# Residual stream with tokens on partitions, tokens stationary in all linears but the mixers' inputs, seven products in part of both MLP matmuls

## The chip, the core and the metric

One Trainium2 core runs the whole program: TensorE (PE, with its weight loads as PEld), VectorE (DVE), ScalarE (ACT), GpSimd (POOL) and the DMA queues of SyncE (SP) and ACT. The metric is the device time of one launch in microseconds, the median of three runs. One further execution was profiled; all rows below are of that one.

## The reference

256 tokens of width 2048 go through two layers. Layer 0 mixes with a recurrent unit and a pooling mixer, layer 1 with sparse attention; after each mixer stand an MLP of width 8192 and a gated addition. Everything is float32.

```python
def rmsnorm(x, g):
    y = x * rsqrt(mean(x * x, axis=-1) + EPS)
    return y * g

for i in range(2):
    hn = rmsnorm(h, ln_mix_g[i])
    h = h + (ab_mixer(hn, ...) if i == 0 else nsa_mixer(hn, ...))   # each ends in "@ w_out", 2048 x 2048
    hn = rmsnorm(h, ln_mlp_g[i])
    h = h + square(relu(hn @ mlp_w_up[i])) @ mlp_w_down[i]          # 2048 x 8192, 8192 x 2048
    gate = sigmoid(rmsnorm(h, ln_ple_g[i]) @ ple_w_gate[i])         # 2048 x 2048
    h = h + gate * (p[i] @ ple_w_proj[i])                           # 256 x 2048
return rmsnorm(h, ln_final_g)
```

## The kernel before

**Precision.** A float32 operand is written as a rounded `hi` part and the rest `lo`, and a product is taken as hi·hi + lo·hi + hi·lo in the fast float32 mode. Activations are kept as such pairs (`X(k)`, feature block k on partitions, 256 columns of hi then 256 of lo). Weights arrive raw by DMA, 1 MB a tile (`raw`, three buffers); ACT makes `hi` (L190) and DVE makes `lo` (L197), four buffers each.

**Order.** Nothing is scheduled by a tool. The list `steps` holds the PE's work in order. A step is one half of a raw tile: 2 x 512 columns of weights for 128 rows each. `run` goes through the steps. At step s it first issues the conversions to `hi` up to s+2, then the PE's matmuls of s, then whatever other code has put down with `after(n, f)` for this step (n steps after the one that called it), then the conversions to `lo` up to s+2. Every engine works through its own queue in that order, so an instruction put down by `after(0, ...)` stands ahead of `lo` of step s+2 in DVE's queue.

**Linears.** `linear` keeps a block of 128 x 128 weights stationary and streams tokens: per block one matmul of `hi` weights over 512 columns (hi and lo of the tokens, L284) and one of `lo` weights over 256 (L285), or in packed groups three of 256 (L280). Its results have features on partitions, as has the residual `h`; `Sums` adds the two halves of a bank, and `residual`, `gate_done` and `up` bring them into `h`, `X` and `H`. `x_stages` makes the next `X` from `h` with the squares for the norm; `rstd_soon` sums these over partitions with a matmul against ones (L364).

**MLP.** The 8192 hidden features go in four quarters q. `up(q)` makes 2048 hidden features with `linear`. `down(q, n2, B)` multiplies them into one half n2 of the outputs, with tokens stationary and 512 columns of weights streamed (L730 to L732, three matmuls a product: hi·hi, lo·hi, hi·lo); its results have tokens on partitions and are gathered in `D`. A pair p is 256 of the hidden features. Six of the eight pairs of a quarter take eight products, in two steps of four (`plain`). Two pairs, called own pairs (3 and 5, in the last quarter 4 and 6), are done with seven products (Q1, Q2, P3, Q5, P7, P6, P4) in four steps of one, two, two and two; DVE forms their weight sums (L758, L763, L764) and the sums of `H` (L700). Four PSUM banks collect the plain products (Q2, P3, P4, C4), four the own ones. When the second own pair is through, `own_out` brings the own banks together in four parts, `out1` to `out4`, one to four steps later; when pair 7 is through, `plain_out` adds the four plain banks to `D` one step later:

```python
                        if p == own[-1] and what[0][0] == "P6":
                            for d, g in enumerate(own_out):
                                after(1 + d, g)
```

After the last quarter `ends` turns `D` by 32 PE transposes a layer (L823) and adds it to `h`.

**Gated addition.** `ple` projects p[i] (packed), then runs the gate's linear; `gate_done` scales, takes tanh on ACT and adds on DVE, column group by column group. At the end of layer 1 `final_stages` and `finish` normalise and write the output.

## Time and profile before

| | |
|---|---|
| runs | 2317.48, 2317.49, 2317.65 us, median 2317.49 |
| profiled execution | 2317.87 us, its span 2315.9 us, so 1.97 us lie around the span |
| PE busy, matmuls | 2288.9 us (99%), 13218 |
| PE weight loads | 2006.2 us (87%) |
| DVE busy | 1722.1 us (74%) |
| ACT busy | 1238.7 us (53%) |
| DMA | 433.65 MB, 187 GB/s on average |
| PE waits for others, all | 15.0 us, of these 6.4 at the start |
| granted TensorE clock | 0.998 on average |

A busy time is the sum of what the profile gives each instruction; matmuls follow each other before the one ahead has ended, so their durations overlap and their pace is read from the starts. A window row gives busy time of each engine in a stretch and in brackets how many instructions began or ran in it. DVE's instructions overlap their neighbours a little too, so their pace also is read from starts.

### The profile page before, as it was taken

The page shows a single profiled execution, that of the slowest core. Times are in us where ns is not written, and L with a number is a line of the kernel's source. Part 1 is how long each engine was busy: PE and PEld are TensorE (multiplying, and loading weights), DVE is VectorE, ACT ScalarE, POOL GpSimd, SP SyncE. Part 2 cuts the span into 40 slices and gives each one's busy share as a digit, 9 for nine tenths or more (in the row PEclk, how much of TensorE's full clock was granted, in tenths as well). Part 3 has the DMA queues.
Part 4 walks back from the last instruction along what each step waited for, and adds up shares of the span by engine and source line. Part 5 has one row for each costly group of instructions (what it writes and reads, how often), then busy time and mean ns, then how long its engine had stood idle before and what let it go on. Part 6 is the DMA issues. An engine that isn't in the chain of part 4 may idle for free.

```text
span 2315.9 us, 33830 instructions
## 1 busy us (share of the span) xinstructions
PE 2288.9 (99%) x13218; PEld 2006.2 (87%) x13218; DVE 1722.1 (74%) x2660; ACT 1238.7 (53%) x1889; POOL 21.7 (1%) x44
## 2 busy tenths in 40 slices
PE   8999999999999999999999999999999999999997
PEld 8998988888888888899889988888888888888896
DVE  6786778768768768977875676767767767857977
ACT  6664555445544545665564555545445445445565
POOL 2000000000000000000000000000000000000000
PEclk9999999999999999999999999999999999999999
DMA  7445455555555555555775224555555555555453
GB/s 261 170 164 194 176 199 200 199 184 200 191 191 196 188 191 187 172 198 203 261 267 182 82 83 165 199 187 191 202 189 184 201 192 187 200 186 194 167 200 110
DMA packets 73360, 433.65 MB, mean 187 GB/s; under 512 B 9968, under 2 KB 18544, under 8 KB 23536
## 3 DMA queue, kind: packets, MB, share of 16 engines
q1 hardware_dynamic: 68640, 426.99, 52.1%
q10 hardware_dynamic: 4560, 4.51, 0.6%
q8 instruction: 103, 1.69, 0.3%
q14 instruction: 57, 0.47, 0.1%
HBM read 429.37 MB, written 2.10 MB: 186 GB/s over the span
## 4 chain that ended last, share of the span: by engine, by line
PE 96%; DVE 2%; issue 0%; ACT 0%; DMA 0%; SPq 0%; DVEq 0%; ACTq 0%
PE ps L284 30%; PE ps L280 17%; PE ps L285 15%; PE ps L732 9%; PE ps L731 9%; PE ps L730 9%; PE ps L1160 1%; PE ps L950 1%; DVE lo L197 1%; DMA raw<-in_ab_w_in 0%; PE ps L1102 0%; PE ps L1100 0%; PE ps L562 0%; PE ps L493 0%; PE ps L1103 0%
## 5 line engine op out<-in xcount | busy, mean ns | idle before, releaser
L190 ACT ACTIVATE hi<-raw 128x1024 fp32r<-128x1024 f32 (+2 forms) x825 | 842.1, 1024 | 756.2 <-PE ps L284 387.0
L197 DVE TENSOR_TENSOR lo<-raw,hi 128x1024 fp32r<-128x1024 f32 (+2 forms) x825 | 964.1, 1178 | 366.3 <-ACT hi L190 365.3
L284 PE MATMUL ps<-big,hi 128*128 128x512 f32 x3008 | 1059.7, 398 | 0.0
L285 PE MATMUL ps<-big,lo 128*128 128x256 f32 x3008 | 841.3, 280 | 0.7 <-DVE lo L197 0.5
L284 PEld LDWEIGHTS ps<-big,hi 128*128 128x128 f32 x3008 | 564.8, 188 | 137.0
L285 PEld LDWEIGHTS ps<-big,lo 128*128 128x128 f32 x3008 | 567.1, 189 | 2.4 <-DVE lo L197 1.5
L280 PE MATMUL ps<-big,hi 128*128 128x256 f32 x2304 | 426.1, 287 | 6.4 <-ACT hi L190 6.4
L732 PE MATMUL ps<-lo,big 128*128 128x512 f32 x992 | 386.3, 389 | 3.1 <-DVE lo L197 3.1
L730 PE MATMUL ps<-hi,big 128*128 128x512 f32 x992 | 386.8, 390 | 0.0
L731 PE MATMUL ps<-hi,big 128*128 128x512 f32 x992 | 386.0, 389 | 0.0
L280 PEld LDWEIGHTS ps<-big,hi 128*128 128x128 f32 x2304 | 362.0, 192 | 8.7 <-ACT hi L190 6.4
L280 PE MATMUL ps<-big,lo 128*128 128x256 f32 x1152 | 327.3, 284 | 2.6 <-DVE lo L197 2.6
L280 PEld LDWEIGHTS ps<-big,lo 128*128 128x128 f32 x1152 | 221.2, 192 | 3.7 <-DVE lo L197 3.6
L732 PEld LDWEIGHTS ps<-lo,big 128*128 128x128 f32 x992 | 186.2, 188 | 42.6 <-DVE lo L197 3.9
L730 PEld LDWEIGHTS ps<-hi,big 128*128 128x128 f32 x992 | 186.2, 188 | 38.6
L731 PEld LDWEIGHTS ps<-hi,big 128*128 128x128 f32 x992 | 186.2, 188 | 38.2
L190 ACT ACTIVATE hi<-T 128x1024 fp32r<-128x1024 f32 x64 | 67.9, 1061 | 103.1 <-PE ps L731 99.2
L197 DVE TENSOR_TENSOR lo<-T,hi 128x1024 fp32r<-128x1024 f32 x64 | 78.1, 1223 | 58.8 <-ACT hi L190 58.8
L308 ACT ACTIVATE t<-ps 128x256 f32<-128x256 f32 x156 | 57.9, 371 | 31.2 <-PE ps L285 31.2
L321 DVE TENSOR_TENSOR t<-ps,t 128x256 f32<-128x256 f32 x156 | 65.4, 419 | 1.5 <-ACT t L308 1.5
L386 ACT ACTIVATE big<-t 128x256 fp32r<-128x256 f32 x136 | 54.4, 401 | 6.7 <-DVE t L687 3.8
L687 DVE SCALAR_TENSOR_TENSOR t<-t 128x256 f32<-128x256 f32 x128 | 54.4, 425 | 4.4
(205 smaller groups left out, 1317.3 us busy)
## 6 DMA issues: line engine op xcount, KB each, us to landing
raw<-in_mlp_w_up SPq DMA_DIRECT2D x128, 1024.0 KB, 4.8
raw<-in_mlp_w_down SPq DMA_DIRECT2D x128, 1024.0 KB, 4.7
raw<-in_c_w_in SPq DMA_DIRECT2D x36, 1024.0 KB, 4.9
raw<-in_ple_w_gate SPq DMA_DIRECT2D x28, 1024.0 KB, 4.9
raw<-in_ab_w_in SPq DMA_DIRECT2D x20, 1024.0 KB, 4.8
raw<-in_ab_w_out SPq DMA_DIRECT2D x16, 1024.0 KB, 4.7
raw<-in_c_w_out SPq DMA_DIRECT2D x16, 1024.0 KB, 4.8
raw<-in_c_cmp_w_k SPq DMA_DIRECT2D x8, 1024.0 KB, 4.8
```

What stands on the lines that cost most here:

```text
L190: act.activation(halves[s]["hi"][:, k, :w], halves[s]["src"][:, k, :], AF.Copy)
L197: dve.tensor_tensor(lo[:, k, :w], src[:, k, :], halves[s]["hi"][:, k, :w].bitcast(F32), op=OP.subtract)
L280: pe.matmul(b, lhsT=wt[:, kk, cols], rhs=x[:, x0:x0 + T], start=first and n == 0 and j % 2 == 0, stop=last and n == 2, skip_group_check=True)
L284: pe.matmul(b, lhsT=hi[:, kk, cols], rhs=x, start=first, stop=False, skip_group_check=True)
L285: pe.matmul(b[:, T:], lhsT=lo[:, kk, cols], rhs=x[:, :T], start=False, stop=last, skip_group_check=True)
L308: act.activation(self.t[j], self.banks[j][:, T:], AF.Copy)
L321: dve.tensor_tensor(dst, self.banks[j][:, :T], self.t[j], op=OP.add)
L386: act.activation(dst[:, :T], src, AF.Copy, **kw)
L687: dve.scalar_tensor_tensor(ts.t[j], ts.t[j], 0.0, ts.t[j], op0=OP.max, op1=OP.mult)
L730: pe.matmul(b, lhsT=x_hi, rhs=hi[:, n, :], start=r not in begun, stop=False, skip_group_check=True)
L731: pe.matmul(b, lhsT=x_lo, rhs=hi[:, n, :], start=False, stop=False, skip_group_check=True)
L732: pe.matmul(b, lhsT=x_hi, rhs=lo[:, n, :], start=False, stop=end, skip_group_check=True)
```

## The change

`h` now has tokens on partitions (`[128, 2, 2048]`), and every linear but the mixers' input projections is done as `down` was: tokens stationary, 512 weight columns streamed, by `mm_set`, one call for each half n2 of 2048 output columns. The mixers' output projections, the gate and the projection of p use plain pairs only. Both MLP matmuls use own pairs, now 2 and 3 of each set of eight, in the order `ORDER` = 0, 1, 4, 5, 2, 6, 3, 7. `D` is gone: `h_out` adds each set's results to `h` right away, scaled by the per-token factor `R2`. What feeds the next matmul has to be turned: `x_after` turns `h` into `X`, `up_out` turns the squared hidden values, and for the first half the sums of its own pairs, into `H` and `S`, by PE transposes (`turn`, `s_back`). The norms' sums come from ACT's squares with an accumulated sum instead of DVE additions and a matmul. In `plain` the loops over n and t are exchanged. The weights are stored in the new blocks, the DMAs stay 1 MB each; `x` is also loaded a second time, 2 MB in the new layout on ACT's queue at step 20, and the final gains once, spread to all partitions.

```diff
--- before.py
+++ after.py
...
+    def mm_set(src, order, X, post, own=(), S=None, between={}, hooks={}):
...
+        def plain(p, k):
+            def fn(hi, lo):
+                for n in range(2):
+                    for t in range(2):
+                        product(PLAIN[t][n], A(p, k, t), hi, lo, n, k == 1 and p == order[-1])
+                if k == 1 and p == order[-1]:
+                    post(w.get("w"), [[acc_of(PLAIN[t][n]) for n in range(2)] for t in range(2)])
+            return fn
...
+                    if p == owned[-1] and what[0][0] == "P6":
+                        for d, g in enumerate((out1, out2, out3)):
+                            after(d, g)
...
+            return [(0, 1, None, fn(("Q1", lambda: A(p, 0, 0)))),
+                    (2, 2, None, fn(("Q2", lambda: A(p, 1, 0)), ("P3", 4))),
+                    (0, 2, first, fn(("Q5", 1), ("P7", 3))),
+                    (0, 2, second, fn(("P6", 2), ("P4", lambda: A(p, 1, 1))))]
...
+        def out1():
...
+            dve.tensor_tensor(w1[:, 1], acc_of("P6"), w1[:, 0], op=OP.subtract)
...
+        def out2():
+            w1, w2 = w["w"]
+            dve.scalar_tensor_tensor(w2[:, 0], w2[:, 0], -1.0, w1[:, 1], op0=OP.mult, op1=OP.subtract)
+            dve.tensor_tensor(w1[:, 1], w1[:, 1], w2[:, 1], op=OP.subtract)
...
+        def out3():
+            w1, w2 = w["w"]
+            dve.scalar_tensor_tensor(w2[:, 1], w2[:, 0], -1.0, w2[:, 1], op0=OP.mult, op1=OP.subtract)
...
+            parts = own_fns(p) if p in own else [(0, 2, None, plain(p, 0)), (2, 2, None, plain(p, 1))]
...
+    def turn(banks, i, of):
+        b = scratch(banks, i)
+        for j in range(2):
+            for t in range(2):
+                pe.transpose(b[:, j, t * P:(t + 1) * P], of(t, i // 2, (2 * i + j) % 4), ident)
...
+    SUM_PAIRS = (2, 3)
+    ORDER = (0, 1, 4, 5, 2, 6, 3, 7)
+    def h_out(n2, r, X, gi, sx=None, w_first=True):
+        def post(w, banks):
...
+            def wide(t):
...
+                    dve.scalar_tensor_tensor(ht, w[t], r[:, t:t + 1], ht, op0=OP.mult, op1=OP.add)
...
+            def adds(n):
+                for t in range(2):
...
+                        dve.scalar_tensor_tensor(hb(t, n), banks[t][n], r[:, t:t + 1], hb(t, n), op0=OP.mult, op1=OP.add)
+            if w is not None:
+                after(0, lambda: (wide(0), wide(1)))
+            after(0, lambda: adds(0))
+            after(0, lambda: adds(1))
+            if X is not None:
+                x_after(n2, banks, X, gi, sx)
...
+    def x_after(n2, banks, X, gi, sx=None, at=0):
...
+        def back(n):
+            for i in (2 * n, 2 * n + 1):
+                turn(banks, i, lambda t, n, c: hb(t, n)[:, c * P:(c + 1) * P])
...
+        def high(i):
...
+                split_hi(X(k), scratch(banks, i)[:, j], scale=gain(k))
...
+        def low(i):
...
+                dve.scalar_tensor_tensor(X(k)[:, T:], scratch(banks, i)[:, j], gain(k), X(k)[:, :T].bitcast(F32),
+                                         op0=OP.mult, op1=OP.subtract)
...
+        for n in range(2):
+            after(at + 1 + n, lambda n=n: back(n))
+            for i in (2 * n, 2 * n + 1):
+                after(at + 1 + n, lambda i=i: high(i))
+                after(at + 2 + n, lambda i=i: low(i))
+            after(at + 2 + n, lambda n=n: squares(n))
+        if sx is not None and n2 == 0:
+            after(at + 2, lambda: (keep(2), keep(3)))
+            after(at + 4, sums)
+            after(at + 5, s_high)
+            after(at + 5, s_low)
...
+            mm_set(lambda p, n2=n2: w[n2][p], order, Y, h_out(n2, None, X, gi, LazyS(0)))
...
+        def up_out(q, n2):
+            def post(w, banks):
+                W = w or wtiles()
...
+                def adds(n):
+                    for t in range(2):
+                        if w:
+                            dve.tensor_tensor(W[t][:, n], banks[t][n], W[t][:, n], op=OP.add)
...
+                def relu(n):
+                    for t in range(2):
+                        act.activation(W[t][:, n], W[t][:, n] if w else banks[t][n], AF.Relu)
+                    for t in range(2):
+                        act.activation(W[t][:, n], W[t][:, n], AF.Square)
...
+                def back(n):
+                    for i in (2 * n, 2 * n + 1):
+                        turn(banks, i, lambda t, n, c: W[t][:, n, c * P:(c + 1) * P])
...
+                def high(i):
+                    k = 2 * i
+                    act.activation(Hs[n2][:, k:k + 2, :T], scratch(banks, i), AF.Copy)
...
+                def low(i):
+                    k = 2 * i
+                    dve.tensor_tensor(Hs[n2][:, k:k + 2, T:], scratch(banks, i), Hs[n2][:, k:k + 2, :T].bitcast(F32),
+                                      op=OP.subtract)
...
+                def sums():
...
+                def s_back(i):
...
+                        pe.transpose(b[:, o], ph["f"][:, i, o], ident)
...
+                def s_split(i):
...
+                for n in range(2):
+                    after(n, lambda n=n: (adds(n), relu(n)))
+                    after(1 + n, lambda n=n: back(n))
+                    for i in (2 * n, 2 * n + 1):
+                        after(2 + n, lambda i=i: high(i))
+                        after(2 + n, lambda i=i: low(i))
+                if n2 == 0:
+                    after(3, sums)
+                    for i in range(2):
+                        after(4, lambda i=i: s_back(i))
+                        after(5, lambda i=i: s_split(i))
...
+        for q in range(4):
+            for n2 in range(2):
...
+                mm_set(lambda p, q=q, n2=n2: a["mlp_w_up"][l][q][n2][p], ORDER, X, post, SUM_PAIRS, LazyS(0))
+            for n2 in range(2):
+                mm_set(lambda p, q=q, n2=n2: a["mlp_w_down"][l][n2][8 * q + p], ORDER, H,
+                       h_out(n2, R2, Xn if q == 3 else None, G_PLE + 16 * l), SUM_PAIRS, LazyS(1))
...
-        def own_pairs(q):
-            return (3, 5) if q < 3 else (4, 6)
...
-                stages(4, [ts.copy, put, lambda j: split_hi(H(j0 + j), ts.t[j]), lambda j: split_lo(H(j0 + j), ts.t[j])],
-                       at=1)
...
-            linear(W("mlp_w_up", l), q * D, [4] * 4, X, done, packed=[0] if q == 0 else [])
...
-                    for t in range(2):
-                        for n in range(2):
-                            r = PLAIN[t][n]
-                            product(r, A(p, k, t), hi, lo, n, k == 1 and p == last[r])
-                    if k == 1 and p == KD // 2 - 1:
-                        after(1, plain_out)
...
-                        if p == own[-1] and what[0][0] == "P6":
-                            for d, g in enumerate(own_out):
-                                after(1 + d, g)
...
-                        dve.tensor_tensor(Dn(t)[:, n], Dn(t)[:, n], acc_of(PLAIN[t][n]), op=OP.add)
-                if q == 3:
+                        act.activation(e[:, t, n2 * 1024 + n * 512:n2 * 1024 + (n + 1) * 512], banks[t][n], AF.Copy, scale=0.5)
...
+        def gate(n2):
+            def post(w, banks):
+                W = wtiles()
...
+                def tanh(n):
+                    for t in range(2):
+                        act.activation(W[t][:, n], banks[t][n], AF.Tanh, scale=HALF[:, t:t + 1])
...
+                def add(n):
+                    for t in range(2):
+                        e = st["e"][:, t, n2 * 1024 + n * 512:n2 * 1024 + (n + 1) * 512]
+                        dve.scalar_tensor_tensor(W[t][:, n], W[t][:, n], 1.0, e, op0=OP.add, op1=OP.mult)
+                        dve.tensor_tensor(hb(t, n), hb(t, n), W[t][:, n], op=OP.add)
+                for n in range(2):
+                    after(at, lambda n=n: tanh(n))
+                    after(at, lambda n=n: add(n))
+                if l == 0:
+                    x_after(n2, banks, Xn, G_MIX + 16, at=at)
...
-                    ends(n2, [acc_of(r) for r in PLAIN[0] + PLAIN[1]])
...
-            def tanh(j):
-                act.activation(ts.t[j], ts.t[j], AF.Tanh, scale=0.5)
...
-            def add(j):
-                hk = h[:, j0 + j, :]
-                dve.scalar_tensor_tensor(ts.t[j], ts.t[j], 1.0, st["e"][:, j0 + j, :], op0=OP.add, op1=OP.mult)
-                dve.scalar_tensor_tensor(hk, ts.t[j], 0.5, hk, op0=OP.mult, op1=OP.add)```

In the orders below `lo<-raw,hi` is one conversion of a raw tile's half, `lo<-T,hi` or `lo<-big,hi` one of a weight sum.

DVE at the end of a `down` set before: the last `lo<-T` belong to the second own pair; L789 and L790 are `out2`, L793 and L794 `out3`, L798 `out4`, L804 `plain_out`; `w_3907` is the buffer `w`.

```order
L197 TENSOR_TENSOR lo<-T,hi 128x1024 x2
L197 TENSOR_TENSOR lo<-raw,hi 128x1024 x3
L789 TENSOR_TENSOR u<-ps,u 128x512
L790 SCALAR_TENSOR_TENSOR w_3907<-w_3907,u 128x512
L197 TENSOR_TENSOR lo<-raw,hi 128x1024
L793 TENSOR_TENSOR u<-u,w_3907 128x512
L794 SCALAR_TENSOR_TENSOR w_3907<-w_3907 128x512
L197 TENSOR_TENSOR lo<-raw,hi 128x1024
L798 TENSOR_TENSOR big<-big,u 128x1024
L798 TENSOR_TENSOR big<-big,w_3907 128x1024
L197 TENSOR_TENSOR lo<-raw,hi 128x1024
L804 TENSOR_TENSOR big<-big,ps 128x512 x4
```

DVE at the same place now: L210 is the conversion to `lo`, L760 is in `out1`, L764 and L765 are `out2`, L769 `out3`, L809 `wide`, L816 `adds`.

```order
L210 TENSOR_TENSOR lo<-big,hi 128x1024 x2
L210 TENSOR_TENSOR lo<-raw,hi 128x1024
L760 TENSOR_TENSOR u<-ps,u 128x512
L210 TENSOR_TENSOR lo<-raw,hi 128x1024
L764 SCALAR_TENSOR_TENSOR big<-big,u 128x512
L765 TENSOR_TENSOR u<-u,big 128x512
L210 TENSOR_TENSOR lo<-raw,hi 128x1024
L769 SCALAR_TENSOR_TENSOR big<-big 128x512
L809 SCALAR_TENSOR_TENSOR h<-u,rs,h 128x1024
L809 SCALAR_TENSOR_TENSOR h<-big,rs,h 128x1024
L816 SCALAR_TENSOR_TENSOR h<-ps,rs,h 128x512 x4
L210 TENSOR_TENSOR lo<-raw,hi 128x1024 x7
```

The first reader of the own banks stood behind three conversions after the own pair's; now it stands behind one, and everything up to the additions into `h` lies ahead of the third conversion after it.

DVE at the end of a gate set now (L1003 and L1004 are `add`, L845 makes the low part of the next `X`):

```order
L210 TENSOR_TENSOR lo<-raw,hi 128x1024 x5
L1003 SCALAR_TENSOR_TENSOR u<-u,big 128x512
L1004 TENSOR_TENSOR h<-h,u 128x512
L1003 SCALAR_TENSOR_TENSOR big<-big 128x512
L1004 TENSOR_TENSOR h<-h,big 128x512
L1003 SCALAR_TENSOR_TENSOR u<-u,big 128x512
L1004 TENSOR_TENSOR h<-h,u 128x512
L1003 SCALAR_TENSOR_TENSOR big<-big 128x512
L1004 TENSOR_TENSOR h<-h,big 128x512
L210 TENSOR_TENSOR lo<-raw,hi 128x1024 x2
L845 SCALAR_TENSOR_TENSOR big<-ps,gains,big 128x256 x4
```

Before, the gate's additions of 256 columns each (L867, L868) stood with one conversion between every two or three of them; now eight of 512 columns stand together ahead of one.

PE at the end of an `up` set (L703 to L705 are the three matmuls of a product, L787 the transposes):

```order
L703 MATMUL ps<-hi,big 128x512
L704 MATMUL ps<-hi,big 128x512
L705 MATMUL ps<-lo,big 128x512
L787 MATMUL ps<-ident,u 128x128
L787 MATMUL ps<-ident,big 128x128
L787 MATMUL ps<-ident,u 128x128
L787 MATMUL ps<-ident,big 128x128
L787 MATMUL ps<-ident,u 128x128
L787 MATMUL ps<-ident,big 128x128
L787 MATMUL ps<-ident,u 128x128
L787 MATMUL ps<-ident,big 128x128
L703 MATMUL ps<-hi,big 128x512
```

Eight transposes stand between two steps, and twice so at the end of each set that is turned; before, `up` had none.

## Rows read from the trace of the kernel before

**Rows 1.** The page: PE over the span, granted clock by fortieths of it

```profile
PE 2288.9 (99%) x13218; PEld 2006.2 (87%) x13218; DVE 1722.1 (74%) x2660; ACT 1238.7 (53%) x1889; POOL 21.7 (1%) x44
...
PEclk9999999999999999999999999999999999999999
```

**Rows 2.** Windows, a quarter's up, then its down: busy us (instructions), clock, DMA

```profile
428.59:519.03 90.44, 90.44 (x514) 78.39 (x512) 57.84 (x82) 42.58 (x59) 0.00 (x0) 1.00 0.54 193
519.03:603.38 84.35, 84.35 (x375) 69.83 (x374) 70.62 (x81) 45.01 (x54) 0.00 (x0) 1.00 0.55 192
```

**Rows 3.** Timeline of PE in a packed group: start, us, instruction

```profile
2285.55 0.28 PE L280 MATMUL ps<-big,lo 128*128 128x256 f32 x1
...
2285.91 0.28 PE L280 MATMUL ps<-big,lo 128*128 128x256 f32 x1
```

**Rows 4.** Timeline of PE at four transposes after a down set

```profile
919.45 0.60 PE L823 MATMUL ps<-ident,big 128*128 128x128 f32 x4
919.80 0.48 PE L730 MATMUL ps<-hi,big 128*128 128x512 f32 x1
920.12 0.40 PE L731 MATMUL ps<-hi,big 128*128 128x512 f32 x1
```

**Rows 5.** Timeline of PE in attention, the third and last of eight transposes

```profile
1392.72 0.27 PE L1140 MATMUL ps<-ident,big 128*128 128x128 f32 x1
...
1393.27 0.27 PE L1145 MATMUL ps<-ident,big 128*16 128x128 f32 x1
```

**Rows 6.** Timeline of DVE at the end of a down set

```profile
1791.30 0.69 DVE L790 SCALAR_TENSOR_TENSOR w<-w,u 128x512 f32<-128x512 f32 x1
1791.91 1.22 DVE L197 TENSOR_TENSOR lo<-raw,hi 128x1024 fp32r<-128x1024 f32 x1
1793.04 0.69 DVE L793 TENSOR_TENSOR u<-u,w 128x512 f32<-128x512 f32 x1
1793.76 0.69 DVE L794 SCALAR_TENSOR_TENSOR w<-w 128x512 f32<-128x512 f32 x1
1794.37 1.22 DVE L197 TENSOR_TENSOR lo<-raw,hi 128x1024 fp32r<-128x1024 f32 x1
1795.51 1.22 DVE L798 TENSOR_TENSOR big<-big,u 128x1024 f32<-128x1024 f32 x1
...
1798.91 1.28 DVE L804 TENSOR_TENSOR big<-big,ps 128x512 f32<-128x512 f32 x2
```

**Rows 7.** DVE groups by shape, without and with a per-partition scalar: mean ns

```profile
L687 DVE SCALAR_TENSOR_TENSOR t<-t 128x256 f32<-128x256 f32 x128 | 54.4, 425 | 4.4
...
L353 DVE SCALAR_TENSOR_TENSOR big<-h,gains,big 128x256 fp32r<-128x256 f32 x80 | 38.1, 479 | 0.0
```

**Rows 8.** Timeline of DVE: an instruction that waits for the transposes of rows 4

```profile
920.09 0.69 DVE L829 TENSOR_TENSOR big<-ps,rstd 128x512 f32<-128x512 f32 x1 [0.49 <-PE ps L823]
```

**Rows 9.** Timeline of DVE where PE waits for `lo`

```profile
936.07 1.22 DVE L197 TENSOR_TENSOR lo<-raw,hi 128x1024 fp32r<-128x1024 f32 x1
```

**Rows 10.** PE at that place

```profile
935.39 0.39 PE L731 MATMUL ps<-hi,big 128*128 128x512 f32 x1
937.34 0.50 PE L732 MATMUL ps<-lo,big 128*128 128x512 f32 x1 [1.56 <-DVE lo L197]
```

**Rows 11.** Window around that place

```profile
930.00:960.00 30.00, 28.44 (x139) 23.77 (x138) 29.29 (x39) 16.81 (x21) 0.00 (x0) 1.00 0.53 170
```

**Rows 12.** ACT group: copies of a bank of 512 columns

```profile
L786 ACT ACTIVATE w<-ps 128x512 f32<-128x512 f32 x32 | 17.2, 595 | 0.0
```

**Rows 13.** Timeline of the last 16 us

```profile
2300.84 0.28 PE L280 MATMUL ps<-big,lo 128*128 128x256 f32 x1
...
2302.53 0.42 DVE L868 SCALAR_TENSOR_TENSOR h<-t,h 128x256 f32<-128x256 f32 x1
...
2305.62 1.75 DVE L1224 RECIPROCAL t<-t 128x256 f32<-128x256 f32 x1 [2.67 <-ACT t L1223]
2307.41 4.70 DVE L1228 TENSOR_TENSOR big<-big,t 128x512 f32<-128x512 f32 x5
```

More of the change, by code (lines that the diff above doesn't have):

```diff
@@ L374, in rstd_soon, with mean_square, r2_of, rstd_of @@
         after(at + 1, second)
+    MS, R2, RSTD, HALF = (rs[:, i, :] for i in range(4))
+    def mean_square():
+        dve.tensor_reduce(MS, ssq, axis=mybir.AxisListType.X, op=OP.add)
+    def r2_of():
+        mean_square()
+        dve.tensor_scalar(R2, MS, 1.0 / D, EPS, op0=OP.mult, op1=OP.add)
+        dve.reciprocal(R2, R2)
+    def rstd_of():
+        mean_square()
+        act.activation(RSTD, MS, AF.Sqrt, scale=1.0 / D, bias=epsb)
+        dve.reciprocal(RSTD, RSTD)
+        dve.tensor_scalar(HALF, RSTD, 0.5, None, op0=OP.mult)
+    def spread(st, key):
+        dg = ttile().rearrange("p (t n) -> p t n", n=P)
+        for t in range(2):
+            dve.tensor_scalar(dg[:, t], ident, RSTD[:, t:t + 1], None, op0=OP.mult)
+        b = bank()
+        pe.matmul(b[:, :T], lhsT=ones, rhs=dg.rearrange("p t n -> p (t n)"), start=True, stop=True)
+        st[key] = sm.tile([P, T], F32, name="rstd", bufs=2)
+        act.activation(st[key], b[:, :T], AF.Copy)
     def new_x(n=16):
@@ new lines, in out_sets, with __init__, __getitem__, split @@
+    def out_sets(w, order, Y, X, gi, mid):
+        for n2 in range(2):
+            if n2:
+                add_hook(mid)
+                add_hook(tools)
+            mm_set(lambda p, n2=n2: w[n2][p], order, Y, h_out(n2, None, X, gi, LazyS(0)))
+    class LazyS:
+        def __init__(self, i):
+            self.i = i
+        def __getitem__(self, at):
+            return ph["S"][self.i][at]
+    def ple_load(l):
+        pst = utile()[:, :2, :]
+        nc.scalar.dma_start(pst, a["pT"][l])
+        def split():
+            for k in range(2):
+                split_hi(ph["pT"][:, k, :], pst[:, k, :])
+                split_lo(ph["pT"][:, k, :], pst[:, k, :])
+        after(4, split)
@@ L877, in trunk @@
+        add_hook(load_e)
+        for n2 in range(2):
+            mm_set(lambda p, n2=n2: a["ple_w_gate"][l][n2][p], range(8), X, gate(n2), between={5: lambda n2=n2: proj(n2)},
+                   hooks={5: rstd_of} if n2 == 0 else {})
+        add_hook(ph["close"])
     X1 = new_x()
-    linear(a["ab_w_out"], 0, [4] * 4, Y, residual(X1, G_MLP), order=[*range(8, 16), *range(8)])
-    add_hook(l0.close)
+    begin()
+    out_sets(a["ab_w_out"], [*range(4, 8), *range(4)], Y, X1, G_MLP, mid=l0.close)
@@ L912, in done @@
             if which == 0:
[L913 removed]
+                after(0, lambda: spread(at, "rstd"))
                 at["blkt"] = big(F32, (P, 4, 32, NC))
@@ L1193, in trunk @@
     X4 = new_x()
[L1194 to L1195 removed]
+    begin()
+    out_sets(a["c_w_out"], range(8), O, X4, G_MLP + 16, mid=l1.close)
     X5 = new_x()
     mlp(1, X4, X5)
[L1200 to L1229 removed]
     ple(1, X5, None)
```

426 lines of the change are left out of this document (194 added, 232 removed).

## The prediction

> **What bounds the kernel now.** I read the page first: PE is busy for 2288.9 of 2315.9 us and its clock stands at the top digit, its 2.4 GHz level, in every fortieth of the span [rows 1]. So the time is what PE has to do plus what little it waits, and an edit counts by the PE time that it removes or adds and by any new wait of PE. PE's pace comes from the windows, which are cut at a quarter's `up` and `down`: 90.44 us for the 256 blocks of an `up`, 0.3533 us a block; 84.35 us for the 372 matmuls of a `down` (two sets of six pairs of 24 and two own pairs of 21), 0.2267 us a matmul [rows 2]. A packed block takes 0.36 us, the distance of two `lo` matmuls [rows 3]. The windows also show how near the second engine is: in `down`, DVE is busy 70.62 of 84.35 us, in `up` 57.84 of 90.44 [rows 2]. The change makes `up` like `down` and adds turning to it, so what matters next is when DVE's work falls. The timelines show that.
>
> **PE's work, part by part.**
> Up: a quarter costs two sets of 186 matmuls, 84.35 us, in place of 90.44. But its results have to be turned: 2 x 16 transposes for `H` and 8 for the sums, 40. Four transposes push the matmul after the next one 0.67 us from the first transpose's start, where a matmul's pace is 0.23: 0.44 us, 0.111 each [rows 4]; in a run of eight they also start 0.11 apart (five gaps in 0.55 us) [rows 5]. 40 x 0.111 = 4.4, so a quarter gains 90.44 - 84.35 - 4.4 = 1.66 us, and eight quarters 13.2. The first quarter's packed group had 64 blocks at 0.36 instead of 0.3533: 0.4 a layer, 0.9 more.
> The mixers' output linears: 32 steps of 12 matmuls, 87.05, and 32 transposes, 3.6, against 90.44: 0.2 lost each, 0.3 together.
> Gate: half of its blocks were packed, 128 x 0.3533 + 128 x 0.36 = 91.3. Layer 0 needs 87.05 + 3.6, a gain of 0.7; layer 1 is not turned, a gain of 4.2. The projections go from 32 x 0.36 = 11.5 to 48 x 0.2267 = 10.9, 1.3 for both.
> Down: the same matmuls, and 32 transposes a layer as before: nothing.
> Sum: 13.2 + 0.9 - 0.3 + 0.7 + 4.2 + 1.3 = 20.0 us less of PE work. The 4608 more matmuls of 512 columns and 416 more transposes nearly eat the 2688 pairs and 1344 packed matmuls that go.
>
> By the Trainium skill's page "TensorE: Matmul & The Clock Gate", section "Part 4: PE-mode transpose", a full transpose takes some 275 ns within a kernel. The rows agree if this is how long one takes (0.27 us), not how far apart they start, 0.11 [rows 5]. If 0.275 were the pace, the sum above would turn from a gain of 20 into a loss of some 48; I take the pace.
>
> **Two waits that go.** PE waits 1.56 us for `lo` where the turned `D` of a layer's last quarter is brought into `h` [rows 10], once a layer, 3.1 together. There DVE is busy 29.29 of 30 us [rows 11], and the `lo` in question ends at 937.29, 0.05 us before PE goes on [rows 9, 10]. That work is now spread otherwise, and I count the 3.1 as gone. It is also the model for what follows: DVE works in order, and once it is behind, PE stands at the third matmul of a product (hi·lo), which alone needs `lo`.
>
> **A wait that comes: the end of each down set.** Before, `out2` was the first DVE work that reads the own banks, and pairs 6 and 7 were still to come; the chain to `plain_out` reached over six steps. Now the second own pair is last but one. `out1`'s subtraction needs P6, so DVE stands until P6's third matmul is through, with `lo` of steps s, s+1 and s+2 behind it (s is the set's last step). From there I lay DVE's queue against PE, both in paces. DVE, from the starts of the same kinds of instructions [rows 6]: 0.61 after an instruction of 512 columns, 0.72 when the next needs its result, 1.13 after one of 1024. `out1` 0.61, `lo` s 1.13, `out2` 0.72 + 0.61, `lo` s+1 1.13, `out3` 0.61, `wide` twice, `adds` four times, `lo` s+2 1.22 to its end. `wide` and `adds` are now scalar_tensor_tensor with a per-partition scalar, which no row shows at these sizes; at 256 columns the scalar costs 0.054 us [rows 7]. With it `wide` is 1.19 and `adds` 0.66 (without it 1.13 and 0.60). Sum 11.05 us. DVE starts 0.20 after PE's pace is through with the matmul: the last of four transposes starts at 919.78, ends its pace at 919.89, and its waiter starts at 920.09 [rows 4, 8]. PE meanwhile does P4's three matmuls, three steps of 2.72 and the first two matmuls of s+2: 0.68 + 8.16 + 0.45 = 9.29. So `lo` comes 0.20 + 11.05 + 0.05 - 9.29 = 2.0 us late. Twelve sets: 24.1. In the four sets of the last quarters eight transposes, 0.89, stand ahead of s+2 and use the wait: 1.1 each, 4.5. Together 28.6. Bounds: nothing, if DVE were not held at P6; 2.9 a set if DVE's instructions followed each other by their full durations, 12 more in all. Sixteen sets make this the largest single term.
>
> The ends of the up sets have the same `out` chain but no `wide`, and only two `adds` before `lo` s+2: 0.2 + 0.61 + 1.13 + 1.33 + 1.13 + 0.61 + 1.2 + 1.22 = 7.4 of 9.29 us. The first transposes wait for ACT's relu and square of two halves: DVE's first additions end some 5.7 and 6.3 us after P6, four ACT passes of 512 columns at about 0.6 [rows 12] bring 8.2, and PE gets there at 8.84. I take 0; bounds 0 and 1 us a set, 16 together.
>
> **Gate sets.** tanh and eight additions are put down for the last step itself. The first bank is done 2.04 us before the set's end; + 0.2 + 0.6 for tanh [rows 12] + 0.1 to DVE, which then needs 4 x (0.72 + 0.61) = 5.3, and 1.22 for `lo` s+2: it is there 5.4 us after the set's end. PE needs it after 3.17, in layer 0 after eight transposes, 4.06. Layer 1's first set loses 2.3, layer 0's two sets 1.4 each: 5.1.
>
> **Tail.** Before, the last product starts at 2300.84, its `h` is done at 2302.95, the five scalings start at 2307.41, 1.75 us of it a reciprocal over 256 columns [rows 13]. Now the last additions end 4.2 us after the last product, and the reciprocal is over two columns; the scalings are about 4.7 again. + 2.2 - 1.7 = 0.5 us.
>
> The second load of `x`, 2 MB, falls where the DMA engines are about half busy (0.54 in such linears) [rows 2] and weights are fetched three tiles ahead: 0. Accumulated squares, relus and copies lie on ACT, busy 42.58 of 90.44 us in `up` [rows 2]: 0, where nothing waits for them.
>
> **Sum.** - 20.0 - 3.1 + 28.6 + 5.1 + 0.5 = + 11.1. The profiled execution has a span of 2315.9 and took 2317.87, which becomes 2329.0; the median of the runs is 0.4 below it, so 2328.6 us.
>
> **Rivals.**
> (1) Faster: the chain at a down set's end costs PE nothing. For it: `lo` is made two steps ahead, and the same chain never held PE in fourteen of the sixteen down ends before. Against: it stood behind three conversions then, not one, and P6 was long done. It would decide if DVE's 11.05 us were under 9.0. Then the waits of 28.6 go, and mostly the gate's too: 2329 - 34 = 2295. Break-even is at (20.0 + 3.1 - 5.6)/16 = 1.1 us a set.
> (2) About half of it, 1 us a set: 2314, no change or little faster.
> (3) The up sets are late too, since relu and square on ACT stand ahead of `hi` of step s+3 and PE's transposes wait for them: 16 sets x 1 us, 2345. For it: the spare time is only 0.6 us there. Against: paces of [rows 6] were used with no gap left out.
> (4) Transposes go at their duration, 0.27 in place of 0.111: 416 x 0.16 = 67 us, 2396. This is what the skill's figure would make of it, in a sentence of its own above; [rows 4, 5] speak against it.
>
> **Chances.** Forecast (2319 to 2338) 0.53; rival 1 0.22; rival 2 0.10; rival 3 0.12; rival 4 0.03. The range from 2293 to 2350 takes in rivals 1 to 3 in their middle. A measurement of this kernel tells 0.2%, 4.6 us, from no change: 2312.9 to 2322.1. Faster: rival 1 and a little of 2, 0.24; within: most of 2 and the forecast's low end, 0.14; slower: the rest, 0.62.
>
> **What would show it.** In the profile after, PE's waits should name `lo` at the third matmul of a product some 19 times, about 2 us each in `down`, 1.1 in the last quarters; DVE's `out1` should show idle time released by PE; an `up` quarter without waits should take 88.8 us; transposes should start 0.11 apart. I am wrong if PE's waits in `down` stay under 1 us a set, if PE also stands at the transposes of `up`, or if the clock falls under its top level after the waits; after the 1.56 us it did not [rows 11].

## The result

The changed kernel takes 2343.55 us (median of four runs, 2337.95 to 2344.5); the kernel before, on the same chip, 2317.48. The ratio is 1.0108, interval 1.009 to 1.0125: slower by 26 us, 1.1%. The sum of the prediction was + 11.1; the sign came out as forecast, less than half of the size did, and the time lies above the forecast range. The profiled execution has a span of 2341.4 us, 25.5 more than before, so the sum was 14.4 short; its own time is 2343.47. (Two executions in experiments 5 and 8, of 2901.54 and 8239.83 us, were disturbed as a whole and stand in no comparison.)

The page of the changed kernel, busy time of PE and DVE and the line of the granted clock, to be laid beside [rows 1]:

```profile
span 2341.4 us, 30197 instructions
...
PE 2283.6 (98%) x11510; PEld 1933.2 (83%) x11510; DVE 1738.2 (74%) x2360; ACT 1314.3 (56%) x1900; POOL 15.5 (1%) x42
...
PEclk9999999999999999999999999999999999999998
```

PE is busy for 5.3 us less than before (2283.6 against 2288.9) while the span is 25.5 longer. So the added time is not more work for PE; most of it is time in which PE stands, and some, as shown below, time in which PE goes at half its pace. The list of waits says where (what waited, for what: us in total, times, longest):

```profile
PE ps L705 <- DVE lo L210: 31.3, 18, 2.1
...
DVE u L760 <- PE ps L705: 26.2, 30, 0.9
```

L705 is the third matmul of a product, the one that needs `lo`; L760 is the subtraction of `out1` that needs P6. The first down set's end, on DVE and then on PE (start, duration, instruction, idle time before it and who ended it):

```profile
379.37 0.69 DVE L760 TENSOR_TENSOR u<-ps,u 128x512 f32<-128x512 f32 x1 [0.87 <-PE ps L705]
379.98 1.22 DVE L210 TENSOR_TENSOR lo<-raw,hi 128x1024 fp32r<-128x1024 f32 x1
381.11 0.69 DVE L764 SCALAR_TENSOR_TENSOR big<-big,u 128x512 f32<-128x512 f32 x1
381.90 0.69 DVE L765 TENSOR_TENSOR u<-u,big 128x512 f32<-128x512 f32 x1
382.51 1.22 DVE L210 TENSOR_TENSOR lo<-raw,hi 128x1024 fp32r<-128x1024 f32 x1
383.65 0.69 DVE L769 SCALAR_TENSOR_TENSOR big<-big 128x512 f32<-128x512 f32 x1
384.25 1.28 DVE L809 SCALAR_TENSOR_TENSOR h<-u,rs,h 128x1024 f32<-128x1024 f32 x1
385.44 1.28 DVE L809 SCALAR_TENSOR_TENSOR h<-big,rs,h 128x1024 f32<-128x1024 f32 x1
386.64 2.73 DVE L816 SCALAR_TENSOR_TENSOR h<-ps,rs,h 128x512 f32<-128x512 f32 x4
389.27 4.63 DVE L210 TENSOR_TENSOR lo<-raw,hi 128x1024 fp32r<-128x1024 f32 x4
```

```profile
388.17 0.39 PE L704 MATMUL ps<-hi,big 128*128 128x512 f32 x1
390.55 0.70 PE L705 MATMUL ps<-lo,big 128*128 128x512 f32 x1 [1.99 <-DVE lo L210]
391.05 0.63 PE L703 MATMUL ps<-hi,big 128*128 128x512 f32 x1
391.48 0.63 PE L704 MATMUL ps<-hi,big 128*128 128x512 f32 x1
...
394.30 0.40 PE L705 MATMUL ps<-lo,big 128*128 128x512 f32 x1
394.53 0.40 PE L703 MATMUL ps<-hi,big 128*128 128x512 f32 x1
```

From `out1`'s start to the end of the `lo` that PE needs (389.27 + 1.22) DVE takes 11.12 us; the prediction laid out 11.05 for the same queue. PE's matmuls start 2.38 us apart here (388.17 to 390.55) instead of 0.23: 2.15 lost, and about 0.12 more until it is at pace again, the refill. This gap of 2.38 stands at all twelve down ends of quarters 0 to 2; at the four of the last quarters it is 1.39.

The second thing to see is what follows. From 391.05 the matmuls start 0.43 apart, nearly twice the usual 0.23, up to 394.04. Four such stretches, called falls below, stand before the last matmul, from 390.7, 749.1, 1646.8 and 2278.3; the windows of the first and the last (from:to, length, busy time of PE, PEld, DVE, ACT, POOL, granted clock, DMA share, GB/s):

```profile
390.75:394.05 3.30, 3.30 (x9) 2.56 (x9) 3.15 (x3) 0.00 (x0) 0.00 (x0) 0.50 0.77 243
...
2278.40:2281.60 3.20, 3.20 (x8) 2.52 (x9) 2.69 (x3) 2.37 (x3) 0.00 (x0) 0.50 0.70 225
```

0.50 is the lower level, 1.2 GHz. Each stretch follows a wait of PE: the first three a down end, the fourth the end of layer 1's first gate set. Eight matmuls 0.2 us late make some 1.65 us each, 6.6 together; this is an estimate, and a little high by the two `down` windows below, which differ by 1.54. The page's line of the clock hides the falls, since a fortieth of the span is 59 us long and a 9 stands for 90% and more. In windows of 320 us one fall makes 0.99; the kernel before reads 1.00 in all of them from 10 to 2250 us, so it had none there. The mean clock of the run of 2337.95 us is 0.997, that of the three others 0.995: so probably it had fewer.

The windows that answer [rows 2]: an `up` quarter, a `down` with one wait and one fall, a `down` with one wait only:

```profile
1507.70:1596.49 88.79, 88.79 (x414) 73.96 (x412) 72.84 (x91) 54.43 (x78) 0.00 (x0) 1.00 0.55 189
1596.49:1686.47 89.98, 87.99 (x390) 72.53 (x388) 69.35 (x74) 49.54 (x59) 0.00 (x0) 0.98 0.54 187
1775.79:1864.23 88.44, 86.45 (x390) 71.40 (x388) 69.29 (x74) 49.56 (x59) 0.00 (x0) 1.00 0.54 190
```

The `up` is 88.79, where 88.8 was given. A `down` without wait would be 84.35 + 16 x 0.111 = 86.1 (the second up set's transposes fall into it); with a wait of 2.28 it is 88.4. Eight transposes in a row on PE and the matmul behind them, answering [rows 4, 5]:

```profile
1514.04 1.03 PE L787 MATMUL ps<-ident,h 128*128 128x128 f32 x8
1514.83 0.48 PE L703 MATMUL ps<-hi,big 128*128 128x512 f32 x1
```

One lasts 0.27; eight in 1.03 leave 0.76 for seven distances, 0.109 each. The tail, answering [rows 13]:

```profile
2325.71 0.39 PE L705 MATMUL ps<-lo,big 128*128 128x512 f32 x1
...
2329.53 0.69 DVE L1004 TENSOR_TENSOR h<-h,big 128x512 f32<-128x512 f32 x1
...
2332.95 4.86 DVE L1036 SCALAR_TENSOR_TENSOR h<-h,rs,big 128x1024 f32<-128x1024 f32 x4
```

From the last matmul to the span's end it is 15.7 us; before it was 15.1 (+ 0.6; forecast + 0.5).

### The profile page after: what moved, and what is told of

It is laid out like the page before. It is cut to its first block, busy times and chain, and to the rows that moved or that the text cites. A ratio compares the mean times of both kernels' runs of the same rounds, so it can differ in the third digit from the quotient of the medians.

```text
span 2341.4 us, 30197 instructions
## 1 busy us (share of the span) xinstructions
PE 2283.6 (98%) x11510; PEld 1933.2 (83%) x11510; DVE 1738.2 (74%) x2360; ACT 1314.3 (56%) x1900; POOL 15.5 (1%) x42
## 4 chain that ended last, share of the span: by engine, by line
PE 94%; DVE 4%; issue 1%; DMA 1%; ACT 0%; SPq 0%; DVEq 0%; ACTq 0%
PE ps L705 24%; PE ps L703 24%; PE ps L704 24%; PE ps L293 10%; PE ps L297 3%; PE ps L787 2%; DVE lo L210 2%; PE ps L298 1%; PE ps L1328 1%; PE ps L1118 1%; DVE h L816 1%; DMA raw<-in_ab_w_in 1%; PE ps L1270 0%; PE ps L1268 0%; DVE h L1004 0%
## 5 line engine op out<-in xcount | busy, mean ns | idle before, releaser
L210 DVE TENSOR_TENSOR lo<-raw,hi 128x1024 fp32r<-128x1024 f32 (+1 forms) x817 | 937.9, 1166 | 228.8 <-ACT hi L203 227.2
L203 ACT ACTIVATE hi<-raw 128x1024 fp32r<-128x1024 f32 (+1 forms) x817 | 818.4, 1014 | 504.3 <-PE ps L704 396.1
L705 PE MATMUL ps<-lo,big 128*128 128x512 f32 x2496 | 976.3, 391 | 31.3 <-DVE lo L210 31.3
L703 PE MATMUL ps<-hi,big 128*128 128x512 f32 x2496 | 979.7, 393 | 0.0
L704 PE MATMUL ps<-hi,big 128*128 128x512 f32 x2496 | 973.7, 390 | 0.0
L705 PEld LDWEIGHTS ps<-lo,big 128*128 128x128 f32 x2496 | 469.9, 188 | 136.7 <-DVE lo L210 38.9
L704 PEld LDWEIGHTS ps<-hi,big 128*128 128x128 f32 x2496 | 470.4, 188 | 96.0
L703 PEld LDWEIGHTS ps<-hi,big 128*128 128x128 f32 x2496 | 470.2, 188 | 95.4
L293 PE MATMUL ps<-big,hi 128*128 128x256 f32 x1408 | 264.0, 289 | 7.2 <-ACT hi L203 7.2
L210 DVE TENSOR_TENSOR lo<-big,hi 128x1024 fp32r<-128x1024 f32 x128 | 156.6, 1223 | 136.8 <-ACT hi L203 136.8
L203 ACT ACTIVATE hi<-big 128x1024 fp32r<-128x1024 f32 x128 | 135.8, 1061 | 215.6 <-PE ps L704 201.7
L293 PEld LDWEIGHTS ps<-big,hi 128*128 128x128 f32 x1408 | 222.7, 193 | 9.2 <-ACT hi L203 7.2
L293 PE MATMUL ps<-big,lo 128*128 128x256 f32 x704 | 200.4, 285 | 2.5 <-DVE lo L210 2.5
L293 PEld LDWEIGHTS ps<-big,lo 128*128 128x128 f32 x704 | 135.6, 193 | 3.3 <-DVE lo L210 3.3
L297 PE MATMUL ps<-big,hi 128*128 128x512 f32 x320 | 113.6, 398 | 0.0
L298 PE MATMUL ps<-big,lo 128*128 128x256 f32 x320 | 89.7, 280 | 0.7 <-DVE lo L210 0.5
L297 PEld LDWEIGHTS ps<-big,hi 128*128 128x128 f32 x320 | 60.1, 188 | 14.1
L298 PEld LDWEIGHTS ps<-big,lo 128*128 128x128 f32 x320 | 60.3, 189 | 2.0 <-DVE lo L210 1.5
L409 ACT ACTIVATE big<-ps,gains 128x256 fp32r<-128x256 f32 x80 | 31.3, 474 | 49.5 <-PE ps L787 49.5
```

Of the source, the lines that this page charges most:

```text
L203: act.activation(halves[s]["hi"][:, k, :w], halves[s]["src"][:, k, :], AF.Copy)
L210: dve.tensor_tensor(lo[:, k, :w], src[:, k, :], halves[s]["hi"][:, k, :w].bitcast(F32), op=OP.subtract)
L293: pe.matmul(b, lhsT=wt[:, kk, cols], rhs=x[:, x0:x0 + T], start=first and n == 0 and j % 2 == 0, stop=last and n == 2, skip_group_check=True)
L297: pe.matmul(b, lhsT=hi[:, kk, cols], rhs=x, start=first, stop=False, skip_group_check=True)
L298: pe.matmul(b[:, T:], lhsT=lo[:, kk, cols], rhs=x[:, :T], start=False, stop=last, skip_group_check=True)
L409: act.activation(dst[:, :T], src, AF.Copy, **kw)
```

## The experiments

The theory to test: the slowdown is waits of PE for `lo`, each a plain sum over DVE's queue, and stretches at the lower clock that come behind some of these waits; without them the change saves PE work. Rivals: the turning or the additional matmuls cost more than the rows of before showed; ACT or the burst into `h` alone is late; the clock falls have nothing to do with the waits.

**1. Own pairs earlier.**

```
-    ORDER = (0, 1, 4, 5, 2, 6, 3, 7)
+    ORDER = (0, 1, 4, 2, 5, 3, 6, 7)
```

> Edit: the own pairs stand fourth and sixth in every set of the MLP, so two plain pairs (eight... four steps of 2.72 us) follow the last P6, as in the kernel before; nothing is added or left out. Theory (DVE held at P6 at the end of a down set, with lo behind it, makes PE wait 12 x 2.28 + 4 x 1.40 = 33.0 us; and the clock falls, some 6.6 us in the profiled execution, come from these waits): waits at the ends of down go, clock at its top level throughout, 2343.5 - 33.0 - 6.6 = 2304 us (2301 to 2308), faster than before. Rival A (the additional transposes and matmuls on PE are what costs): no change, 2340 to 2346. Rival B (the clock falls have nothing to do with these waits): 2310.5, with about four half-rate stretches of 3.4 us left. Rival C (the six instructions that bring a set into h, 5 us in one burst, are late by themselves, wherever the own pairs stand): about half of the waits stay, 2320 to 2327.

Measured: 2304.46 us (2303.53 to 2305.77, four runs), before 2317.36; ratio 0.9945, interval 0.993 to 0.9959. The waits for `lo` that are left (the first line) are at gate ends; DVE at the same down end:

```profile
PE ps L705 <- DVE lo L210: 3.4, 2, 2.1
```

```profile
419.92 0.69 DVE L769 SCALAR_TENSOR_TENSOR big<-big 128x512 f32<-128x512 f32 x1
420.52 2.35 DVE L210 TENSOR_TENSOR lo<-raw,hi 128x1024 fp32r<-128x1024 f32 x2
422.79 1.28 DVE L809 SCALAR_TENSOR_TENSOR h<-u,rs,h 128x1024 f32<-128x1024 f32 x1
...
427.82 3.48 DVE L210 TENSOR_TENSOR lo<-raw,hi 128x1024 fp32r<-128x1024 f32 x3
```

`out3` is through early and two `lo` stand between it and the burst into `h`, so nothing is late. All 16 waits are gone and with them every fall (windows of 320 us from 10 to 2250 us all read 1.00), in the profiled execution even behind the gate's 2.53 us gap. The span falls by 39.9 us: 12 x 2.28 + 4 x 1.4 + 6.6 = 39.6. Rivals A and C (PE work; the burst alone) are out, and B (falls without waits) has nothing left to stand on here.

**2. The same order, the burst taken apart.**

```
-                after(0, lambda: (wide(0), wide(1)))
-            after(0, lambda: adds(0))
-            after(0, lambda: adds(1))
+                after(0 if X is not None else 1, lambda: (wide(0), wide(1)))
+            after(0 if X is not None else 2, lambda: adds(0))
+            after(0 if X is not None else 3, lambda: adds(1))
```

> Edit: the own pairs stay second to last; in quarters 0 to 2 the six instructions that bring a down set into h are put down one, two and three steps later (wide, adds of the first half, adds of the second half). Theory (what is late is the sum of out chain and burst in one piece: 0.20 + 11.05 + 0.05 - 9.29 = 2.0 us): DVE then needs 0.2 + 0.61 + 1.13 + 1.33 + 1.13 + 0.61 + 1.22 = 6.2 us up to the lo in question, of 9.29, and later ones have 2 us to spare; the 12 waits of 2.28 us go, the four of the last quarters stay: 2343.5 - 27.4 = 2316, less some clock falls 3 to 6 us, so 2310 to 2316. Rival (DVE standing at P6 is enough by itself to hold lo back): the waits stay, 2340 to 2346.

Measured: 2310.35 us (2309.06 to 2311.15, six runs), ratio 0.9969 (0.9958 to 0.9981). The span is 34.4 shorter than that of the changed kernel: 12 x 2.28 = 27.4, and the 6.6 of clock falls. DVE still stands at P6 in this kernel, 0.88 us at the first down end; so it was the length of the queue behind it, not the standing alone. All four falls went, though four gaps of 1.39, two of 1.6 and one of 2.53 us are still in this execution.

**3. Half of it.** Only the additions of a set's second half one step later, on the changed kernel:

```
-            after(0, lambda: adds(1))
+            after(0 if X is not None else 1, lambda: adds(1))
```

> Edit on the changed kernel: in quarters 0 to 2 only the two additions of a down set's second half are put down one step later. Theory (DVE's lateness is a plain sum, so two additions of 0.66 us less ahead of the lo in question shorten each of the twelve waits from 2.15 to 0.83 us; and at such a wait the clock stays at its top level): 12 x 1.32 = 16 us, and most of the 6.6 us of clock falls, 2343.5 - 16 - 5 = 2322.5 us (2320 to 2326). Rival (a wait of PE is a matter of yes or no, and brings its falls in any case): above 2326, up to 2343.

Measured: 2322.02 us (2321.2 to 2322.92, ten runs), ratio 1.002 (1.0011 to 1.0029). DVE and PE at the first down end:

```profile
386.32 1.40 DVE L816 SCALAR_TENSOR_TENSOR h<-ps,rs,h 128x512 f32<-128x512 f32 x2
387.64 1.21 DVE L210 TENSOR_TENSOR lo<-raw,hi 128x1024 fp32r<-128x1024 f32 x1
388.78 1.40 DVE L816 SCALAR_TENSOR_TENSOR h<-ps,rs,h 128x512 f32<-128x512 f32 x2
```

```profile
387.86 0.39 PE L704 MATMUL ps<-hi,big 128*128 128x512 f32 x1
388.91 0.50 PE L705 MATMUL ps<-lo,big 128*128 128x512 f32 x1 [0.67 <-DVE lo L210]
389.25 0.40 PE L703 MATMUL ps<-hi,big 128*128 128x512 f32 x1
```

The gap is 1.05, so 0.82 lost, where 0.83 was given: a wait is what is left of a sum, and two instructions fewer in the queue shorten it by their 1.32 us. No down end has a fall behind it: windows of 320 us read 1.00 up to 2250 us. The one that the profile shows is behind the gate's gap of 2.53:

```profile
2257.63:2260.60 2.97, 2.97 (x8) 2.30 (x7) 2.86 (x3) 1.97 (x3) 0.00 (x0) 0.50 0.81 262
```

The ten runs fall into two groups, 2321.2 to 2321.6 and 2322.4 to 2322.9, about one fall apart.

**4. Gate additions spread.**

```
-                    after(at, lambda n=n: add(n))
+                    if l == 1 and n2 == 1:
+                        after(at, lambda n=n: add(n))
+                    else:
+                        after(n, lambda n=n: add(n, [0]))
+                        after(n + 1, lambda n=n: add(n, [1]))
```

(with `add` taking the token tiles to add, and `x_after` and the squares one step later)

> Edit: the eight additions of a gate set go two, four and two to the set's last step and the two after it, the turning of layer 0 one step later; the very last set stays as it is. Theory (eight additions of 5.3 us in one piece ahead of lo make PE wait at three gate ends, 1.42 + 1.42 + 2.30): these waits go, 2343.5 - 5.1 = 2338 (2336 to 2340), 1.6 less still where the clock fall after the third goes with it. Rival (ACT's tanh is what is late): no change, 2342 to 2345.

Measured: 2335.45 us (2334.11 to 2336.04, four runs), ratio 1.0077 (1.0062 to 1.0092): 8 us off where 5 to 7 were expected. In the profiled executions it is 7.4: the three gate waits, 5.5 with the refill, are gone, and there are three falls instead of four, all at down ends. What is left are the sixteen down ends:

```profile
PE ps L705 <- DVE lo L210: 27.8, 16, 2.0
```

**5. Every transpose of `turn` twice.**

```
-        for j in range(2):
-            for t in range(2):
-                pe.transpose(b[:, j, t * P:(t + 1) * P], of(t, i // 2, (2 * i + j) % 4), ident)
+        for _ in range(2):
+            for j in range(2):
+                for t in range(2):
+                    pe.transpose(b[:, j, t * P:(t + 1) * P], of(t, i // 2, (2 * i + j) % 4), ident)
```

> Edit: every transpose of turn is issued twice into the same place, 416 more. Theory (0.111 us each, what they push the next matmul): 416 x 0.111 = 46 us, of which the six sets with a wait right behind their transposes swallow 0.89 each: + 41, 2384 us (2378 to 2392). Rival (a transpose goes at its duration, 0.275 us): + 114, 2458. Rival (hidden beside matmuls): 2343.

Measured: 2380.37 us (median of three runs, 2380.06 to 2382.43), ratio 1.0276 (1.0256 to 1.0297). One line of the group by shapes (minimum, median, longest ns; the other 576 of the 832 transposes stand in two lines like it):

```profile
L788 PE MATMUL ps<-ident,u x256: 270/272/273, 302.3 to 2173.0; 128*128 128x128 f32 x128
```

From the wait at one down end to that at the end of the next quarter's first set it is 136.72 instead of 133.27 us: 3.45 for 32 more transposes, 0.108 each. At the last quarters' down ends and layer 0's gates no gap over 0.9 us is left: there the transposes fill the wait. That makes 416 x 0.11 = 45.8, less 6 x 0.89 for these, less 3.3 for two falls fewer (two instead of four): 37.2, measured 36.6 in the span. The Trainium skill's page "TensorE: Matmul & The Clock Gate", section "Part 4: PE-mode transpose", gives some 275 ns for a 128x128 bf16 transpose within a kernel; the median here is 272 in float32, and yet one more of them costs PE 0.11. Duration and price are two things.

**6. Both edits, 1 and 4.** The diffs are those two.

> Edit: both of the edits that took waits away, the own pairs fourth and sixth and the gate additions spread over three steps; nothing left out. Theory (the slowdown is waits of PE for lo and what the clock does behind them, on top of a change that saves PE work): 2304.5 with the own pairs moved, less 5.1 us of gate waits, 2299 us (2296 to 2301), and the clock at its top level in every run, so that the runs differ by less than 1 us. Rival (the two edits hide the same loss): 2303 to 2305.

Measured: **2297.88 us** (2297.64 to 2298.94, four runs), ratio to the kernel before 0.9917, interval 0.9902 to 0.9932. The two longest waits of PE for a split weight that are left:

```profile
PE ps L293 <- ACT hi L203: 7.2, 1, 7.2
...
PE ps L298 <- DVE lo L210: 0.5, 1, 0.5
```

The 7.2 us are the start of the program. Windows of 320 us from 10 to 2250 us all read 1.00, so there is no fall; the runs differ by 1.3 us, where less than 1 was expected. This is the best version, 20 us faster than the kernel before and 46 faster than the changed one, with the same number of instructions as the latter on every engine. It says what the change is worth on PE: span 2295.7 against 2315.9. Adding to it the waits of the changed kernel, 33.0 at down ends and 5.5 at gates, and 6.6 of falls gives 2340.8; the trace has 2341.4.

**7. Waits made on purpose.** On the best version, 3, 6 or 2 more DVE instructions at each of the twelve down ends, with results that nobody reads:

```
+            if X is None and w is not None:
+                after(0, lambda: dead(3))
...
+            def dead(k):
+                for j in range(k):
+                    ht = h[:, j % 2, n2 * 1024:(n2 + 1) * 1024].rearrange("p (n c) -> p n c", c=512)
+                    dve.tensor_tensor(w[j % 2], ht, ht, op=OP.add)
```

> Edit on the kernel with both: at the end of each of the twelve down sets of quarters 0 to 2, three more DVE instructions of 1024 columns that write a tile nobody reads any more. DVE there has 1.5 us to spare; 3 x 1.15 - 1.5 = 1.95 us late, 0.12 more until PE is at pace again. Theory (DVE's lateness makes both the wait and the clock falls): 12 x 2.07 = 25, and two to four falls of 1.65 us in a run: 2299 + 25 + 5 = 2329 us (2325 to 2332). Rival (the clock falls belong to the order of the pairs, not to a wait): 2324 with the clock at its top level. Rival (DVE's additional work finds room): 2299.

> Edit: as the one with three, but six such instructions: 6 x 1.15 - 1.5 = 5.4 us late, 5.5 with the refill, twelve times: 66 us. Theory: 2299 + 66 = 2365 and more clock falls than behind the waits of 2 us; if behind each of the twelve one fall of 3.4 us, 12 x 1.65 = 20 more, 2385; so 2370 to 2386. Rival (falls have nothing to do with a wait's length or with waits): 2365 to 2370.

> Edit: as the kernel with three additional DVE instructions at each of twelve down ends, but two. With three the waits were 0.25 us longer than worked out; so 2 x 1.15 - 1.25 = 1.05, with the refill 1.17 us, twelve times: 14. Theory (falls come behind waits of 2 us and more, as with three and six, not behind one of 1 us): 2297.9 + 14 = 2312 us (2310 to 2314), runs within 1.5 us of each other, no stretch at half rate before the last product. Rival (falls come behind any wait, about one in four): 2317 to 2320.

Measured: with 3, 2332.88 us (2331.73 to 2334.02, four runs); with 6, 2396.85 (2396.52 to 2397.45, four runs); with 2, 2314.79 (2314.07 to 2315.09, ten runs). Their waits, in this order:

```profile
PE ps L705 <- DVE lo L210: 26.8, 12, 2.2
```

```profile
PE ps L705 <- DVE lo L210: 67.6, 12, 5.6
```

```profile
PE ps L705 <- DVE lo L210: 13.1, 12, 1.1
```

All three times lie above their expected ranges, by 0.9, 10.9 and 0.8 us: the spare time of DVE was some 1.1 us rather than 1.5 (with 3, PE lost 2.39 a wait; with 2, 1.25 instead of 1.05). The waits are of the size of those of the changed kernel, in another order of the pairs, and the falls come back: three of 3.4 us with 3 instructions (windows from 391.3, 616.6 and 1865.8; the first is shown). With 2 there is none: the four windows below hold the twelve waits, three each, and read 1.00, where the same windows of the kernel with 3 read 0.99, 0.99, 1.00 and 0.99:

```profile
391.30:394.20 2.90, 2.90 (x8) 2.31 (x7) 2.45 (x3) 0.12 (x1) 0.00 (x0) 0.50 0.90 314
```

```profile
380.00:590.00 210.00, 206.74 (x930) 170.67 (x929) 174.02 (x188) 113.25 (x133) 0.00 (x0) 1.00 0.55 192
590.00:800.00 210.00, 206.72 (x930) 170.65 (x929) 173.92 (x188) 114.93 (x137) 0.00 (x0) 1.00 0.56 194
1620.00:1830.00 210.00, 206.74 (x930) 170.65 (x930) 174.64 (x188) 112.72 (x133) 0.00 (x0) 1.00 0.55 193
1830.00:2040.00 210.00, 206.74 (x930) 170.69 (x929) 173.35 (x187) 114.80 (x137) 0.00 (x0) 1.00 0.56 194
```

With none behind twelve waits, and ten runs within 1.0 us of each other, the rival that falls come behind any wait, about one in four, does not hold for waits of this size. With 6, every one of the twelve waits has a fall, and it begins inside the wait (clock 0.88 in the first window, 0.50 in the next):

```profile
388.04:394.06 6.02, 0.38 (x2) 0.00 (x0) 6.02 (x7) 0.80 (x1) 0.00 (x0) 0.88 0.00 0
394.06:399.30 5.24, 5.24 (x12) 4.13 (x13) 3.35 (x3) 0.99 (x1) 0.00 (x0) 0.50 0.83 294
```

Its span is 98.8 us above the best version's; the waits are 12 x 5.9 = 71, and the remaining 28 make 2.3 us a fall. The expected 1.65 was too little, since most of these falls last twice as long. The rivals "falls belong to the order of the pairs" and "falls have nothing to do with a wait's length" are out.

**8. `up` without the seven products**, on the best version:

```
-                mm_set(lambda p, q=q, n2=n2: a["mlp_w_up"][l][q][n2][p], ORDER, X, post, SUM_PAIRS, LazyS(0))
+                mm_set(lambda p, q=q, n2=n2: a["mlp_w_up"][l][q][n2][p], ORDER, X, post)
```

> Edit on the kernel with both: the up sets go without the seven products (all eight pairs plain), as up had it before the change; the turning stays. Sixteen sets of 192 instead of 186 matmuls, at 0.2267 us. Theory (PE's work is the time once no wait is left): 16 x 6 x 0.2267 = 21.8 us more, 2321 us (2318 to 2323), so no faster than the kernel before. Rival (the sums and the recombining on DVE and ACT cost as much as the seven products save): 2297 to 2305.

Measured: 2319.93 us (median of nine runs, 2319.38 to 2320.86), ratio 1.0011 (1.0001 to 1.0021). There is no trace to read here, so only the times speak: 22.1 us more than the best version, where 96 matmuls of 0.2267 make 21.8. This is no faster than the kernel before (2317.38). The seven products in `up` are the whole gain of the best version; the tokens on partitions by themselves, in this form, bring none.

## Why the prediction came out as it did

**Right: the place and the mechanism of the main term.** DVE was held at P6 in every down end, its queue took 11.12 us against 11.05, PE stood at the third matmul, and rival 3 (waits at the transposes of `up`) did not come. Experiments 1, 2, 3 and 7 show the wait as a sum that can be shortened and lengthened by single instructions. That the measured 2343.55 lies beside rival 3's 2345 is chance.

**Right: PE's price list.** A transpose costs 0.108 to 0.109 us where 0.111 was given, an `up` quarter takes 88.79, `up`'s seven products are worth 22.1 us: rival 4 is out, by experiment 5.

**Wrong: the sum has no term for falls of the clock.** This is the step that failed. The prediction names "if the clock falls under its top level after the waits" only as a sign of being wrong and, because "after the 1.56 us it did not [rows 11]", prices it at nothing. I took two waits of before, with gaps of 1.95 us between matmul starts, as evidence for nineteen waits that I myself put at 1.1 to 2.3 us late, which makes gaps of 1.3 to 2.5, most of them longer. Four falls cost 6.6 of the 14.4 us that the sum was short, the largest part; with them it would have given 2335.2. Experiments 1, 2 and 6 take them away by taking the waits away, experiment 3 takes them away at the down ends by making the waits shorter, and experiment 7 brings them back with other waits. It should have stood among the rivals with its price, one fall being some 1.65 us.

**Mis-sized: the wait itself, 33.0 instead of 28.6.** Each end cost 2.28, not 2.0, and 1.4, not 1.1, in the last quarters. Of the 0.28, some 0.12 is the refill: when `lo` comes PE does not go on at its pace at once (in experiment 3, 388.91 to the next matmul's 389.25 is 0.34, not 0.23). The refill was left out of the sum; the rest is DVE's queue, 0.07 longer, and its start, some 0.06 later. The gate ends cost 5.5, given 5.1.

**Mis-sized: PE's work and the tail, 16.5 saved instead of 19.5.** I worked the first quarter of a layer out as 64 blocks of 0.36 and 192 of 0.3533, 90.87 us. A window of before that I had not cut shows 90.03, and so 1.7 less to gain:

```profile
254.21:344.24 90.03, 90.03 (x580) 81.63 (x579) 63.75 (x99) 45.16 (x65) 0.00 (x0) 1.00 0.53 186
...
956.74:969.48 12.74, 12.74 (x110) 12.73 (x108) 11.88 (x16) 8.36 (x15) 0.61 (x2) 1.00 0.68 241
2208.69:2301.07 92.38, 91.89 (x649) 85.83 (x647) 70.60 (x125) 58.49 (x107) 0.00 (x0) 1.00 0.45 149
```

The second window is a projection with 16 transposes, 12.74 - 1.78 = 10.96 instead of 11.52: 1.1 less to gain for two. The third is layer 1's gate, 1.1 more to gain. The first matmul of the program starts 0.75 us later than before. Together 2.5 of the 3.0.

So the tally of the 14.4: falls 6.6, down ends 4.4, gates 0.4, PE work and tail 3.0, less 0.6 because the two waits of before that go were worth 3.7 with their refill, not 3.1; 0.6 has no place.

**Rival 1** (the chain hidden, 2295 us) is what the best version is: 2297.88. The forecast's own condition for it, DVE's queue under 9 us, was met there by putting two plain pairs behind the last P6: from `out1` to the same `lo` it is 6.1 us (in experiment 1, 415.64 to 421.74), since the burst into `h` no longer stands in it.
